# A seven-product FFN block whose two psum banks per unit become two tiles

## The chip, the cores and the metric

The kernel runs on one core of a Trainium2 chip. The metric is the device time of one execution, in microseconds (us). One profiled execution gives the trace; further runs are timed without it.

## What is computed

One backbone layer over 512 latent tokens and 256 context tokens, width 1024, with a feed-forward block (D_FF 2816) ahead of and behind a mixer of gated linear attention and differential attention. All weights are float32. The change lies in the first feed-forward block and in the adaLN modulation that is computed beside it:

```python
ml = jnp.split((jax.nn.silu(c) @ w_ada[i] + b_ada[i])[:, None, :], N_MOD, axis=-1)
mc = jnp.split((jax.nn.silu(c_ctx) @ w_ada[i] + b_ada[i])[None, None, :], N_MOD, axis=-1)

xl = xl + 0.5 * ml[2] * _swiglu(_modnorm(xl, ffn1_norm[i], ml[0], ml[1]), ffn1_w1[i], ffn1_w3[i], ffn1_w2[i])
xc = xc + 0.5 * mc[2] * _swiglu(_modnorm(xc, ffn1_norm[i], mc[0], mc[1]), ffn1_w1[i], ffn1_w3[i], ffn1_w2[i])

def _swiglu(h, w1, w3, w2):
    return (jax.nn.silu(h @ w1) * (h @ w3)) @ w2
```

## The kernel before, in words

A float32 number is split into a high part (rounded, by a copy on ScalarE) and the rest (by a subtraction on VectorE); a product of two split matrices is three matmuls: low by high, high by low, high by high. So each weight tile passes `split_w`: `whi<-raw` on ScalarE, then `wlo<-raw,whi` on VectorE.

**Units.** The 22 tiles of the inner dimension of the first feed-forward block are taken in pairs. The first pair is computed in a plain loop over k (`psum2`, `act_pair`). Each of the ten other pairs gives two units of class `Unit`: `i` = 0 for w1, `i` = 1 for w3, so units 0 to 19, in this order. A unit forms the four outputs of a 2 by 2 block product (two tiles by two token halves of TH = 384) from seven products instead of eight. A product (`prod`) is 12 matmuls of 128x384 into one psum bank. Three banks are in use: `pa` and `pf`, the first 384 columns of bank 0 and of bank 1 of one tile `st` of two banks, and `pe`, a tile of its own. `pa` accumulates and is copied by ScalarE at three points: p1 into `pa`, copy c1; p6 into `pa`, copy c2; p7 into `pa`, copy c3; p4 into `pa`. p5 and p3 go into `pf`, p2 into `pe`. The outputs are out(3) = c3 + `pf` (before p3), out(0) = c1 + `pe`, out(2) from `pa` after p4, and out(1) = c2 + `pf` after p3. For `i` = 0 VectorE adds and ScalarE applies Silu to give `s` (for out(2) ScalarE alone, `s<-st`); for `i` = 1 VectorE adds (`c<-c,st`), multiplies into `s` (`s<-st,s` for out(2)), ScalarE copies `gh<-s` and VectorE forms `gl`, the split gated result.

**What runs beside it.** Units 2, 3, 4, 5, 8, 9, 12, 13, 16 and 17 carry Down work (`Down`, products `dn` of the second weight with finished gated results, four output tiles each): ScalarE scales each result into a tile `yd`, and a DMA on GpSimd's queue adds it to `xs` in DRAM. `ada_dot` (line 129) gives the modulation: a 512 KB row block `adaw` is loaded by SP's queue and VectorE multiplies and sums it, in one or two products of 128x1024; 56 loads, 80 products, some in each Down unit.

**Order.** In a unit without Down work p4, out(2), p3 and out(1) are left to the next unit: p1, p5, then the earlier unit's p4, out(2), p3, out(1), then p6, p2, p7. In a unit with Down work all seven run: p1, p5 (the earlier unit's p4 and p3, if left), p6, Down, p7, Down, p2, p4, p3. Unit matmuls, copies, splits and outputs are kept in program order (`Kept`, the trace shows them all at line 496); the ada products and the loads are placed among them by the scheduler. An engine executes its instructions in order. Dependences are followed tile by tile: an instruction that writes a tile waits for what still reads it, whichever columns or banks the two touch.

The loop over units is at lines 659 to 732; `psum` (541) makes the tile, `out` (585) and `copy` read it, `Down.add` (650) makes `yd`.

Of the kernel before, what the change touches and what calls it, by code (L numbers as in the profile page):

```python
# [10 lines left out]
F32 = mybir.dt.float32  # L11
# [3 lines left out]
AF = mybir.ActivationFunctionType  # L15
ALU = mybir.AluOpType
AX = mybir.AxisListType
PSUM = bass.MemoryType.PSUM
DRAM = bass.MemoryType.DRAM

P = 128
D = 1024
# [3 lines left out]
T = TL + TC  # L26
# [4 lines left out]
TH, LH, CH = T // 2, TL // 2, TC // 2  # L31
# [27 lines left out]
def layer(tc, a, out, dump=None, stop=None):  # L59
    nc = tc.nc  # L60
    V, S, G, PE, SY = nc.vector, nc.scalar, nc.gpsimd, nc.tensor, nc.sync
    es = ExitStack()

    def pool(name, bufs=1, **kw):
        return es.enter_context(tc.tile_pool(name=name, bufs=bufs, **kw))
# [1 line left out]
    cst = pool("cst")  # L67
    wp = pool("wp")
    hp = pool("hp")
    ps = pool("ps", space=PSUM)  # L70
    dr = pool("dr", space=DRAM)

    def big(nm):
        return ps.tile([P, 1024], F32, tag="big", name=nm, bufs=2)

    def sm(nm):
        return ps.tile([P, 512], F32, tag="sm", name=nm, bufs=2)

    def gm(nm):
        return ps.tile([P, 512], F32, tag="gm", name=nm, bufs=2)  # L80

    uid = [0]

    def u(s):
        uid[0] += 1
        return f"{s}{uid[0]}"
# [35 lines left out]


    def ada_dot(pool_, junk, sc, j, which):
        w = pool_.tile([P, D], F32, tag="adaw", name=u("adaw"), bufs=3)
        SY.dma_start(w, a["ada"][j - 16])
        for i in which:
            jk = junk()
            V.scalar_tensor_tensor(jk, w, 1.0, sc[:, i, :], op0=ALU.mult, op1=ALU.mult,  # L129
                                   accum_out=mods[:, j, i:i + 1])  # L130
# [208 lines left out]
    h1 = Parts(B)  # L339
    h1.at = lambda i, k, o0, n: B[k // 4 * 2 + o0 // TH][i][:, k % 4, :]  # L340

    def psum2():
        t = [big(u("h13")) for _ in range(2)]
        return t, [(lambda o0, n, q=q: q[:, o0 // TH * 512:o0 // TH * 512 + TH]) for q in t]

    with tc.tile_pool(name="st", bufs=1) as sp_:
        scT = sp_.tile([P, KT, 32], F32, name="scT")
# [9 lines left out]
        pts, ds = psum2()  # L357
# [64 lines left out]
    def act_pair(f, pts):  # L422

        gh, gl = ring[f]
        s, p1, p3 = sums()[:, :T].rearrange("p (t n) -> p t n", t=2), *[q.rearrange("p (t n) -> p t n", t=2)[:, :, :TH] for q in pts]
        S.activation(s, p1, AF.Silu)
        V.tensor_tensor(s, s, p3, op=ALU.mult)
        S.activation(gh, s, AF.Copy)
        V.tensor_tensor(gl, s, gh.bitcast(F32), op=ALU.subtract)

    def sums():
        return sf.tile([P, D], F32, tag="Y", name=u("Y"), bufs=1)
# [11 lines left out]
    pts, ds = psum2()  # L444
# [64 lines left out]
    class Unit:  # L509
# [29 lines left out]
            self.S4 = split_w(self.a, spare[0][:, :512], spare[0][:, 512:])  # L539

        def psum(self):
            t = big(u("st"))
            self.pa, self.pf, self.pe = t[:, :TH], t[:, 512:512 + TH], sm(u("pe"))[:, :TH]
            if self.i == 0:
                ss[self.p] = sp0.tile([P, 4, TH], F32, tag="s", name=u("s"), bufs=1)
            self.s = ss[self.p]
# [82 lines left out]
    class Down:  # L629
# [20 lines left out]
        def add(self, j):  # L650
            m = self.m0 + j
            w = self.w[m - m % self.mw]
            y = sr.tile([P, 2, TH], F32, tag="yd", name=u("yd"), bufs=2)
            for i, seg in enumerate((LAT, CTX)):
                o_ = down(*CHUNKS1[self.c], w, m % self.mw * self.nf * P, seg, kPE)
                kS.activation(y[:, :, seg[0]], o_, AF.Copy, scale=gate[:, i, m:m + 1])
            G.dma_start(xs[:, m], y, accum_op=ALU.add)
# [77 lines left out]
    ada_bias(5, 9, (0,))  # L735
    ada_es.close()
    sf_es.close()
    V.tensor_scalar(gate[:, 2, :], mods[:, 40:48, 0], 0.5, None, op0=ALU.mult)
    V.tensor_scalar(gate[:, 3, :], mods[:, 64:72, 0], 0.5, None, op0=ALU.mult)
    mod_scale(2, V_MIX, 4, 0)  # L740
# [122 lines left out]
    with tc.tile_pool(name="dqp", bufs=1) as dq:  # L863
# [130 lines left out]
        st = {}  # L994
# [598 lines left out]
```

## Time and profile before

| what | value |
|---|---|
| median of 3 runs | 1896.28 us (1895.37 to 1898.03) |
| profiled execution | 1893.73 us |
| its span | 1891.9 us |
| mean granted TensorE clock | 0.969 |
| TensorE busy | 1738.4 us (92%) |
| VectorE busy | 1106.1 us (58%) |
| ScalarE busy | 750.9 us (40%) |

The units run from 86 to 663 us of the span. A wait is read as the idle time in front of an instruction and what ended it. The granted clock is the share of full speed that the throttle gave TensorE: 1.00 is 2.4 GHz, 0.50 is 1.2 GHz. Of a group of matmuls in a timeline row, "x12" counts those that follow each other without a stop.

### The profile page before, as it was taken

The numbers are of one execution on the slowest core, as the hardware profiler recorded it, in microseconds if no ns is written. First come the engines' busy times: TensorE is split into PE (matmuls) and PEld (weight loads), VectorE is DVE, ScalarE is ACT, GpSimd is POOL, SyncE is SP. The second block draws the span as 40 slices with busy tenths as digits, with TensorE's granted clock in tenths as the row PEclk, the third lists the DMA queues.
The fourth block names the chain that finished last, engine by engine and source line by source line (L and its number), as shares of the span: only waits on it lengthen the run. The fifth ranks groups of instructions, "written<-read, shape, count | busy, mean of one in ns | idle before, by whom it ended". The sixth has DMA issues, their size and how long they took to land.

```text
span 1891.9 us, 25078 instructions
## 1 busy us (share of the span) xinstructions
PE 1738.4 (92%) x9944; PEld 1552.4 (82%) x9944; DVE 1106.1 (58%) x1836; ACT 750.9 (40%) x1172; POOL 154.5 (8%) x244
## 2 busy tenths in 40 slices
PE   6787988878789879999999979999999999999997
PEld 4776877878778768989988879999888988888887
DVE  4775655565454566677765577668656743333335
ACT  4533333333233333455556463434333432222233
POOL 3022000100001021000000022112100200000000
PEclk9899999989899899999999999999999999999999
DMA  9347644636455055433432211211355322333231
GB/s 357 106 146 146 155 116 122 156 113 174 122 162 109 23 186 162 112 90 93 108 101 84 78 34 57 67 57 34 112 172 173 100 80 81 108 85 107 87 113 66
DMA packets 76486, 215.46 MB, mean 114 GB/s; under 512 B 9880, under 2 KB 14232, under 8 KB 75040
## 3 DMA queue, kind: packets, MB, share of 16 engines
q1 hardware_dynamic: 70608, 198.12, 33.3%
q0 software_dynamic: 5760, 15.73, 5.8%
q8 instruction: 78, 1.28, 0.3%
q14 instruction: 40, 0.33, 0.1%
HBM read 175.02 MB, written 27.26 MB: 107 GB/s over the span
## 4 chain that ended last, share of the span: by engine, by line
PE 67%; issue 17%; DVE 6%; DMA 4%; ACT 4%; POOL 2%; SPq 0%; DVEq 0%; ACTq 0%; POOLq 0%
PE h L248 8%; PE pl L248 8%; PE st L496 5%; PE h L245 4%; PE pl L245 4%; PE pb L248 3%; PE ptm L837 3%; PE ptm L836 3%; PE ptm L838 3%; PE S L945 2%; PE dn L496 2%; PE dn L119 2%; PE dn L121 2%; PE dn L120 2%; PE po L248 2%
## 5 line engine op out<-in xcount | busy, mean ns | idle before, releaser
L113 ACT ACTIVATE whi<-raw 128x1024 fp32r<-128x1024 f32 (+3 forms) x182 | 178.3, 983 | 264.5 <-PE dn L121 68.0
L114 DVE TENSOR_TENSOR wlo<-raw,whi 128x1024 fp32r<-128x1024 f32 (+3 forms) x169 | 191.2, 1135 | 151.0 <-ACT whi L113 149.6
L248 PE MATMUL h<-hH,whi 128*128 128x512 f32 (+2 forms) x384 | 145.3, 378 | 0.0
L248 PE MATMUL h<-hL,whi 128*128 128x512 f32 (+2 forms) x384 | 145.0, 378 | 0.0
L245 PE MATMUL h<-hH,wlo 128*128 128x512 f32 (+2 forms) x368 | 139.9, 381 | 1.9 <-ACT hH L401 0.9
L245 PE MATMUL pl<-hH,wlo 128*128 128x512 f32 x328 | 132.0, 402 | 10.0 <-DVE sg L1170 5.5
L248 PE MATMUL pl<-hL,whi 128*128 128x512 f32 x328 | 130.8, 399 | 0.0
L248 PE MATMUL pl<-hH,whi 128*128 128x512 f32 x328 | 130.5, 398 | 0.0
L496 PE MATMUL st<-T,whi 128*128 128x384 f32 x480 | 128.1, 349 | 0.0
L837 PE MATMUL ptm<-wlo,hH 128*128 128x256 f32 x384 | 109.7, 286 | 5.3 <-DVE wlo L114 5.3
L836 PE MATMUL ptm<-whi,hL 128*128 128x256 f32 x384 | 111.0, 290 | 0.0
L496 PE MATMUL st<-T,wlo 128*128 128x384 f32 x240 | 85.9, 358 | 27.3 <-ACT c L496 27.3
L838 PE MATMUL ptm<-whi,hH 128*128 128x256 f32 x384 | 109.4, 285 | 0.0
L496 PE MATMUL dn<-gh,wlo 128*128 128x512 f32 (+1 forms) x288 | 98.7, 343 | 10.0 <-ACT yd L496 10.0
L496 PE MATMUL st<-hC,hH 128*128 128x384 f32 x240 | 57.3, 397 | 50.2 <-DVE s L496 41.1
L129 DVE SCALAR_TENSOR_TENSOR Y<-adaw,sc 128x1024 f32<-128x1024 f32 x80 | 97.8, 1223 | 9.0 <-DMA adaw<-ada 8.1
L496 PE MATMUL dn<-gl,whi 128*128 128x512 f32 (+1 forms) x288 | 98.6, 342 | 1.0 <-DVE gl L496 1.0
L496 PE MATMUL dn<-gh,whi 128*128 128x512 f32 (+1 forms) x288 | 98.2, 341 | 0.0
L496 PEld LDWEIGHTS st<-hC,hH 128*128 128x128 f32 x240 | 49.8, 225 | 56.6 <-DVE s L496 44.3
L496 PEld LDWEIGHTS st<-T,whi 128*128 128x128 f32 x480 | 92.0, 199 | 0.0
L947 ACT ACTIVATE e<-S,st 128x768 f32<-128x768 f32 x64 | 57.6, 901 | 67.9 <-DVE st L946 67.8
L496 ACT ACTIVATE yd<-dn,gate 128x512 f32<-128x512 f32 x80 | 45.5, 580 | 98.1 <-PE dn L496 73.3
(351 smaller groups left out, 4592.2 us busy)
## 6 DMA issues: line engine op xcount, KB each, us to landing
raw<-win SPq DMA_DIRECT2D x65, 512.0 KB, 3.6
adaw<-ada SPq DMA_DIRECT2D x56, 512.0 KB, 4.3
raw<-f2w SPq DMA_DIRECT2D x44, 512.0 KB, 3.5
xs<-yd POOLq DMA_DIRECT2D x40, 384.0 KB, 5.1
raw<-f1w SPq DMA_DIRECT2D x22, 512.0 KB, 4.1
L<-f1w SPq DMA_DIRECT2D x40, 256.0 KB, 3.3
aw<-ada SPq DMA_DIRECT2D x8, 1024.0 KB, 14.5
raw<-wbr SPq DMA_DIRECT2D x16, 512.0 KB, 3.6
```

The lines of the kernel that those rows point to most:

```text
L113: S.activation(hi[:, :w], raw[:, :w], AF.Copy)
L114: ld = (eng or V).tensor_tensor(lo[:, :w], raw[:, :w], hi[:, :w].bitcast(F32), op=ALU.subtract)
L119: PE.matmul(out_, wl, xh, start=first, stop=False)
L120: PE.matmul(out_, wh, xlo, start=False, stop=False)
L129: V.scalar_tensor_tensor(jk, w, 1.0, sc[:, i, :], op0=ALU.mult, op1=ALU.mult, accum_out=mods[:, j, i:i + 1])
L245: PE.matmul(dst(o0, n), wl[:, ks], h.at(0, k, o0, n), start=(k == 0), stop=False)
L248: mm = PE.matmul(dst(o0, n), wh[:, ks], h.at(i, k, o0, n), start=False, stop=(k == KT - 1 and i == 0))
L496: return lambda *x, **y: tc.keep_in_program_order(f(*x, **y))
L836: PE.matmul(o_, tl, wh[:, cs], start=f, stop=False)
L837: PE.matmul(o_, th, wl[:, cs], start=False, stop=False)
L838: PE.matmul(o_, th, wh[:, cs], start=False, stop=l)
L947: S.activation(e[:, c, :], sp[:, :T], AF.Exp, bias=st4[:, c:c + 1], accum_out=st4[:, 2 + c:3 + c])
```

## The change

`bank(tag)` makes tiles of one bank, "ba" and "bf", two buffers each; `psum` of a unit takes `pa` and `pf` from them, and `psum2` of the first pair likewise. The four tags of psum live in a pool `ps1` that is closed behind the units; a new pool `ps` serves the rest of the kernel. `act_pair` works on each token half by itself, since its two banks are no longer one tile. `adaw` has two buffers instead of three, `yd` three instead of two. Names of lines move by four or five (L496 becomes L501, L129 becomes L130).

```diff
--- before.py
+++ after.py
@@ -67,17 +67,18 @@
     cst = pool("cst")
     wp = pool("wp")
     hp = pool("hp")
-    ps = pool("ps", space=PSUM)
+    ps_es = ExitStack()
+    psb = [ps_es.enter_context(tc.tile_pool(name="ps1", bufs=1, space=PSUM))]
     dr = pool("dr", space=DRAM)
 
     def big(nm):
-        return ps.tile([P, 1024], F32, tag="big", name=nm, bufs=2)
+        return psb[0].tile([P, 1024], F32, tag="big", name=nm, bufs=2)
 
     def sm(nm):
-        return ps.tile([P, 512], F32, tag="sm", name=nm, bufs=2)
+        return psb[0].tile([P, 512], F32, tag="sm", name=nm, bufs=2)
 
     def gm(nm):
-        return ps.tile([P, 512], F32, tag="gm", name=nm, bufs=2)
+        return psb[0].tile([P, 512], F32, tag="gm", name=nm, bufs=2)
 
     uid = [0]
 
@@ -122,7 +123,7 @@
 
 
     def ada_dot(pool_, junk, sc, j, which):
-        w = pool_.tile([P, D], F32, tag="adaw", name=u("adaw"), bufs=3)
+        w = pool_.tile([P, D], F32, tag="adaw", name=u("adaw"), bufs=2)
         SY.dma_start(w, a["ada"][j - 16])
         for i in which:
             jk = junk()
@@ -339,9 +340,12 @@
     h1 = Parts(B)
     h1.at = lambda i, k, o0, n: B[k // 4 * 2 + o0 // TH][i][:, k % 4, :]
 
+    def bank(tag):
+        return psb[0].tile([P, 512], F32, tag=tag, name=u(tag), bufs=2)[:, :TH]
+
     def psum2():
-        t = [big(u("h13")) for _ in range(2)]
-        return t, [(lambda o0, n, q=q: q[:, o0 // TH * 512:o0 // TH * 512 + TH]) for q in t]
+        t = [[bank(tag) for tag in ("ba", "bf")] for _ in range(2)]
+        return t, [(lambda o0, n, q=q: q[o0 // TH]) for q in t]
 
     with tc.tile_pool(name="st", bufs=1) as sp_:
         scT = sp_.tile([P, KT, 32], F32, name="scT")
@@ -422,9 +426,10 @@
     def act_pair(f, pts):
 
         gh, gl = ring[f]
-        s, p1, p3 = sums()[:, :T].rearrange("p (t n) -> p t n", t=2), *[q.rearrange("p (t n) -> p t n", t=2)[:, :, :TH] for q in pts]
-        S.activation(s, p1, AF.Silu)
-        V.tensor_tensor(s, s, p3, op=ALU.mult)
+        s = sums()[:, :T].rearrange("p (t n) -> p t n", t=2)
+        for t in range(2):
+            S.activation(s[:, t], pts[0][t], AF.Silu)
+            V.tensor_tensor(s[:, t], s[:, t], pts[1][t], op=ALU.mult)
         S.activation(gh, s, AF.Copy)
         V.tensor_tensor(gl, s, gh.bitcast(F32), op=ALU.subtract)
 
@@ -539,8 +544,7 @@
             self.S4 = split_w(self.a, spare[0][:, :512], spare[0][:, 512:])
 
         def psum(self):
-            t = big(u("st"))
-            self.pa, self.pf, self.pe = t[:, :TH], t[:, 512:512 + TH], sm(u("pe"))[:, :TH]
+            self.pa, self.pf, self.pe = bank("ba"), bank("bf"), sm(u("pe"))[:, :TH]
             if self.i == 0:
                 ss[self.p] = sp0.tile([P, 4, TH], F32, tag="s", name=u("s"), bufs=1)
             self.s = ss[self.p]
@@ -650,7 +654,7 @@
         def add(self, j):
             m = self.m0 + j
             w = self.w[m - m % self.mw]
-            y = sr.tile([P, 2, TH], F32, tag="yd", name=u("yd"), bufs=2)
+            y = sr.tile([P, 2, TH], F32, tag="yd", name=u("yd"), bufs=3)
             for i, seg in enumerate((LAT, CTX)):
                 o_ = down(*CHUNKS1[self.c], w, m % self.mw * self.nf * P, seg, kPE)
                 kS.activation(y[:, :, seg[0]], o_, AF.Copy, scale=gate[:, i, m:m + 1])
@@ -735,6 +739,8 @@
     ada_bias(5, 9, (0,))
     ada_es.close()
     sf_es.close()
+    ps_es.close()
+    psb[0] = pool("ps", space=PSUM)
     V.tensor_scalar(gate[:, 2, :], mods[:, 40:48, 0], 0.5, None, op0=ALU.mult)
     V.tensor_scalar(gate[:, 3, :], mods[:, 64:72, 0], 0.5, None, op0=ALU.mult)
     mod_scale(2, V_MIX, 4, 0)
```

The matmuls of the units stand in the same order as before. What moves is what they wait for, and where the ada products stand on VectorE. In the rows below numbers tell one buffer of a name from another.

TensorE at the end of unit 13 (Down, `i` = 1): p3 of unit 13 into the second bank, then p1 of unit 14. Before:

```order
L496 MATMUL st_3420<-hC_93,hH_91 128x384 [waits DVE_49]
L496 MATMUL st_3420<-hC_93,hH_91 128x384 x11
L496 MATMUL st_3719<-hH_91,wlo_3658 128x384
L496 MATMUL st_3719<-hH_91,whi_3657 128x384 [waits Activation_49]
L496 MATMUL st_3719<-hH_91,whi_3657 128x384
L496 MATMUL st_3719<-hH_91,wlo_3658 128x384
```

and of the changed kernel:

```order
L501 MATMUL bf_3442<-hC_93,hH_91 128x384 [waits DVE_49]
L501 MATMUL bf_3442<-hC_93,hH_91 128x384 x11
L501 MATMUL ba_3741<-hH_91,wlo_3680 128x384 [waits DVE_49]
L501 MATMUL ba_3741<-hH_91,whi_3679 128x384 [waits Activation_49]
L501 MATMUL ba_3741<-hH_91,whi_3679 128x384
L501 MATMUL ba_3741<-hH_91,wlo_3680 128x384
```

p3's wait on VectorE is before for the `s` that out(2) forms from the first bank; now it is for `c` of out(3), the last reader of the second bank, and p1 has got a wait of its own for the weights' `wlo`.

TensorE from the last matmuls of unit 14's p1 into its p5. Before:

```order
L496 MATMUL st_3719<-hH_91,wlo_3658 128x384
L496 MATMUL st_3719<-hH_91,whi_3657 128x384 x2
L496 MATMUL st_3719<-T_564,wlo_3658 128x384 [waits Activation_49]
L496 MATMUL st_3719<-T_565,whi_3657 128x384
L496 MATMUL st_3719<-T_564,whi_3657 128x384
L496 MATMUL st_3719<-T_564,wlo_3658 128x384
L496 MATMUL st_3719<-T_565,whi_3657 128x384
```

and of the changed kernel:

```order
L501 MATMUL ba_3741<-hH_91,wlo_3680 128x384
L501 MATMUL ba_3741<-hH_91,whi_3679 128x384 x2
L501 MATMUL bf_3742<-T_570,wlo_3680 128x384
L501 MATMUL bf_3742<-T_571,whi_3679 128x384
L501 MATMUL bf_3742<-T_570,whi_3679 128x384
L501 MATMUL bf_3742<-T_570,wlo_3680 128x384
L501 MATMUL bf_3742<-T_571,whi_3679 128x384
```

p5 (`T,wlo` and on) waited for ScalarE's copy c1 of the first bank and now waits for nothing; p6, which follows p5 here and writes the first bank, waited for nothing and now waits for c1 and for its weights.

VectorE at the end of unit 11 (left over into unit 12, which has Down work): out(2) into `s`, out(1) into `c` and `s`, the splits `hC`, `hH` of the unit's weights, with the ada products `Y<-adaw` between. Before:

```order
L129 SCALAR_TENSOR_TENSOR Y_3327,mods<-adaw_3325,sc 128x1024 [waits DMAHW0_49,DVE_49]
L496 TENSOR_TENSOR wlo_3130<-raw_3104,whi_3129 128x1024 [waits DMAHW2_49,PE_49,Activation_49]
L129 SCALAR_TENSOR_TENSOR Y_3331,mods<-adaw_3329,sc 128x1024 [waits DMAHW1_49,DVE_49]
L129 SCALAR_TENSOR_TENSOR Y_3365,mods<-adaw_3363,sc 128x1024 [waits DMAHW2_49,DVE_49]
L129 SCALAR_TENSOR_TENSOR Y_3369,mods<-adaw_3367,sc 128x1024 [waits DMAHW3_49,DVE_49]
L496 SCALAR_TENSOR_TENSOR s_2875<-st_2970,s_2875 128x384 [waits PE_49]
L496 TENSOR_TENSOR hC_93<-L_2973,hL_92 128x1024 [waits Activation_49]
L496 TENSOR_TENSOR gl_3098<-s_2875,gh_3097 128x384 [waits DVE_49]
L496 TENSOR_TENSOR c_3053<-c_3053,st_2970 128x384 [waits PE_49]
L496 TENSOR_TENSOR s_2875<-s_2875,c_3053 128x384 [waits DVE_49]
L496 TENSOR_TENSOR hH_91<-A_2974,hH_91 128x512 [waits Activation_49]
L496 TENSOR_TENSOR gl_3078<-s_2875,gh_3077 128x384 [waits DVE_49]
```

and of the changed kernel:

```order
L130 SCALAR_TENSOR_TENSOR Y_3293,mods<-adaw_3291,sc 128x1024 [waits DMAHW7_49,DVE_49]
L501 TENSOR_TENSOR wlo_3151<-raw_3125,whi_3150 128x1024 [waits DMAHW1_49,PE_49,Activation_49]
L501 SCALAR_TENSOR_TENSOR s_2894<-ba_2989,s_2894 128x384 [waits PE_49]
L130 SCALAR_TENSOR_TENSOR Y_3348,mods<-adaw_3346,sc 128x1024 [waits DMAHW0_49,DVE_49]
L501 TENSOR_TENSOR hC_93<-L_2993,hL_92 128x1024 [waits Activation_49]
L501 TENSOR_TENSOR gl_3118<-s_2894,gh_3117 128x384 [waits DVE_49]
L501 TENSOR_TENSOR c_3073<-c_3073,bf_2990 128x384 [waits PE_49]
L130 SCALAR_TENSOR_TENSOR Y_3352,mods<-adaw_3350,sc 128x1024 [waits DMAHW1_49,DVE_49]
L501 TENSOR_TENSOR s_2894<-s_2894,c_3073 128x384 [waits DVE_49]
L130 SCALAR_TENSOR_TENSOR Y_3386,mods<-adaw_3384,sc 128x1024 [waits DMAHW3_49,DVE_49]
L501 TENSOR_TENSOR hH_91<-A_2994,hH_91 128x512 [waits Activation_49]
L501 TENSOR_TENSOR gl_3098<-s_2894,gh_3097 128x384 [waits DVE_49]
```

Ada products that stood ahead of out(2)'s `s` now stand behind it, between out(2) and the `gl` of out(1); there are three between them where there were none.

## Rows read from the trace of the kernel before

**Rows 1.** The page's head: span and number of instructions.
```profile
span 1891.9 us, 25078 instructions
```

**Rows 2.** Unit stage: length, busy time (instructions) by engine, granted clock, DMA share, GB/s.
```profile
86.00:663.00 577.00, 485.74 (x2558) 450.86 (x2559) 324.66 (x489) 203.61 (x322) 48.50 (x56) 0.93 0.50 127
```

**Rows 3.** Waits in 86 to 663 us: engine, awaited; us in all, times, longest.
```profile
PE st L496 <- DVE s L496: 41.1, 10, 6.6
...
PE st L496 <- ACT c L496: 27.3, 20, 4.4
...
ACT yd L496 <- DMA xs<-yd: 18.8, 5, 5.6
...
PE dn L496 <- ACT yd L496: 10.0, 7, 3.2
PE st L496 <- ACT s L496: 9.1, 10, 1.2
...
DVE Y L129 <- DMA adaw<-ada: 8.1, 11, 1.4
...
PE st L496 <- DVE c L496: 1.2, 1, 1.2
```

**Rows 4.** Half-clock windows, TensorE: length, busy (instructions), granted clock, DMA share; their sum.
```profile
486.42:489.83 3.41, 3.41 (x9) 0.50 0.76 107
504.28:510.31 6.03, 6.03 (x19) 0.50 0.00 0
...
sum 56.76, PE 56.75; mean PE 4.37
```

**Rows 5.** Timeline, TensorE: start, us, operation, count, idle before and its end.
```profile
552.03 2.37 PE L496 MATMUL st<-hC,hH 128*128 128x384 f32 x12 [2.14 <-DVE s L496]
```

**Rows 6.** Timeline behind unit 13, the same columns.
```profile
503.67 0.55 DVE L496 SCALAR_TENSOR_TENSOR s<-st,s 128x384 f32<-128x384 f32 x1
504.25 0.52 ACT L496 ACTIVATE gh<-s 128x384 fp32r<-128x384 f32 x1 [2.23 <-DVE s L496]
...
504.28 4.21 PE L496 MATMUL st<-hC,hH 128*128 128x384 f32 x12 [6.56 <-DVE s L496]
...
511.50 0.49 ACT L496 ACTIVATE c<-st 128x384 f32<-128x384 f32 x1 [1.27 <-PE st L496]
...
512.05 0.44 PE L496 MATMUL st<-T,wlo 128*128 128x384 f32 x1 [0.58 <-ACT c L496]
```

**Rows 7.** Timeline in unit 4: the first Down weights' low part, the first Down product.
```profile
200.16 1.22 DVE L496 TENSOR_TENSOR wlo<-raw,whi 128x1024 fp32r<-128x1024 f32 x1
...
202.75 0.39 PE L496 MATMUL dn<-gh,wlo 128*128 128x512 f32 x1
```

**Rows 8.** Timeline in unit 12: p5, the last ada product, out(1)'s `gl`, a Down product.
```profile
420.78 0.44 PE L496 MATMUL st<-T,wlo 128*128 128x384 f32 x1 [4.39 <-ACT c L496]
...
428.78 1.23 DVE L129 SCALAR_TENSOR_TENSOR Y<-adaw,sc 128x1024 f32<-128x1024 f32 x1 [1.41 <-DMA adaw<-ada]
...
436.60 0.55 DVE L496 TENSOR_TENSOR gl<-s,gh 128x384 fp32r<-128x384 f32 x1
...
437.76 0.39 PE L496 MATMUL dn<-gh,wlo 128*128 128x512 f32 x1
```

**Rows 9.** The page's groups and DMA issues: the ada products, the loads of `adaw`.
```profile
L129 DVE SCALAR_TENSOR_TENSOR Y<-adaw,sc 128x1024 f32<-128x1024 f32 x80 | 97.8, 1223 | 9.0 <-DMA adaw<-ada 8.1
...
adaw<-ada SPq DMA_DIRECT2D x56, 512.0 KB, 4.3
```

**Rows 10.** Timeline at the stage's end: out(1) of unit 19.
```profile
659.83 0.56 DVE L496 TENSOR_TENSOR c<-c,st 128x384 f32<-128x384 f32 x1 [0.56 <-PE st L496]
```

## The prediction

> **What bounds the kernel now.** I read the page's head first, then busy time by stage, then the waits of the stage that the change touches, then the windows of half clock, then the timeline around the longest waits. The profiled execution spans 1891.9 us [rows 1] and took 1893.73 us, 1.83 us around the span; it lies 2.55 us under the median of the runs, 1896.28 us. The sum is made on the profiled execution and then moved by these 2.55 us.
>
> The change works almost wholly in the unit stage, 86 to 663 us. There TensorE is busy 485.74 of 577 us, VectorE 324.66 and ScalarE 203.61, and the granted clock is 0.93 [rows 2]: no engine is full, so TensorE waits for results, some 91 us in all. The waits say for what [rows 3]: 41.1 us for VectorE's `s` (10 times) and 9.1 us for ScalarE's `s` (10 times), both in front of p3; 27.3 us for ScalarE's copy `c` (20 times), in front of p5; 10.0 us for `yd`, of which ScalarE itself waited 18.8 us for the DMA out of `yd`. The waits of p3 and p5 are waits on the other half of the same tile: p3 writes `pf` in bank 1 while out(2) reads `pa` in bank 0, and p5 writes `pf` while c1 is read from `pa`.
>
> Behind long waits the clock falls. The windows that follow waits of 2.66 us and more stand at a granted clock of 0.50, the lower of the two levels, 1.2 GHz; 13 of them hold 56.76 us of matmuls [rows 4], which at 2.4 GHz would take half, so they cost 28.4 us. The wait of 2.14 us had none behind it: the p3 there took 2.37 us for its twelve matmuls [rows 5], the one at 504.28 took 4.21 [rows 6]. The Trainium skill (TensorE: Matmul & The Clock Gate, "Terms") puts the penalty at throttled time times the share of pulses withheld; with the stage's mean clock of 0.93 [rows 2] that would be some 40 us, an estimate, and the first rival below would end 12 us lower. Against it: in its throttled time lie the waits themselves, in which no matmul is slowed. I stay with the 28.4 us of the busy rows.
>
> **The change part by part, its places in the order of the sum.**
>
> *p5, eleven places.* Twenty p5 waited 27.3 us; four took 4.4 us (17.6 us, one is in [rows 8]), so sixteen share 9.7 us, 0.6 each. Five of these stand behind a Down unit and are counted there. In the changed program c1's copy is needed at p6, a product later, and nothing else of p5's stands behind it. Twelve matmuls at full clock take some 2.1 us, and the copy 0.49 us [rows 6], so p5 hides it. Eleven times 0.6: **6.7 us**.
>
> *p3 of the i = 0 units.* Ten waits on ScalarE's Silu, 9.1 us [rows 3]. Now p3 waits for out(3)'s read of the second bank, which lies before p4. What is late next is p6, a product behind p3: it follows c1, and c1 stood ahead of the Silu. **9.1 us**.
>
> *From a Down unit with i = 1 to the next unit (five places).* Take 497.7 us: p4 has ended, p3 waits 6.56 us for `s`, starts at 504.28, and runs at half clock with the next p1; p5 then waits 0.58 us and starts at 512.05 [rows 6]; p6 could follow 2.1 us later, at 514.1. Why is `s` late? Not for p4: out(2)'s `s` stands on VectorE behind c3, out(3), the split of the next weights, out(0) and the split of Y. That order stays. So after the change TensorE runs p3, p1 and p5 from 497.7 to 504.0 and then stops at p6. p6 writes `pa` over c1's source, and c1 stands on ScalarE behind the `gh` of out(2) and of out(1). The chain from the row at 503.67: `s` to 504.22, `gl` behind `gh` to 505.4, `c` to 506.0 and `s` to 506.5 (p3 is long done), `gh` 0.52 to 507.0, c1 to 507.4. A gap of 3.4 us, and by the 2.66 us above half clock behind it: 3.4 to 6.0 us of matmuls in such windows [rows 4], so 1.7 to 3.0 us; I take 2.0. p6's work is then 514.1 − 507.4 − 2.0 = 4.7 us earlier. I take this for four places. At the fifth Down work follows: its first product needs `wlo`, begun at 200.16, and started at 202.75 [rows 7]; one ada product fewer lies ahead of `wlo` now, so it comes a little over 1 us earlier, to 200.3; less half of a short clock window I take 1.8. Together 4 × 4.7 + 1.8 = **20.6 us** of the 50 us (6.6 + 0.6 + 2.8 of clock, five times) that these places lose now. Bounds: 10 us where a clock window of 6 us stands behind each and c1 is later by 1 us, 35 us where the clock stays.
>
> *From a plain i = 1 unit to a Down unit (four places).* Here three ada products stand ahead of `s`, the last after 1.41 us for its load, and the Down product for the third f tile starts at 437.76, one microsecond after `gl` of out(1) [rows 8]. The waits at p5 (4.4) and at p3 go. But TensorE then arrives at the third tile about 9 us early, at 428.5, and must have that `gl`. On VectorE one to four ada products move from ahead of `s` to behind it, with three still between `s` and `gl`; from the durations (1.31 us each, `hC` 1.2, `hH` 0.7, three of 0.6) `gl` comes to 431 to 434. The gap there is 3 to 5 us, with a clock window behind it of 2 us. Per place 437.8 − 434 − 2.0 = 1.8 at the late end, 4.8 at the early one, and nothing where loads hold the products up. I take 0.5 each, near the bad end for the loads' sake (next part): **2 us**, between −6 and 18.
>
> *adaw with two buffers, yd with three.* A buffer of `adaw` is loaded in 4.3 us and read in 1.22 us [rows 9], 1.31 with the read of the accumulator: three buffers give a load every 1.9 us, two every 2.8. VectorE waited 8.1 us for such loads [rows 3]. Most of what is added meets an idle VectorE (252 us in the stage) and costs nothing; some 3 us of it stand in the chains above, which is why I took their bad end. Behind a waiting product are queued `s`, `gl` and the splits, and TensorE's Down work and next unit wait for these. Loads of `raw`, `L` and `A` stand earlier on SP's queue than before, a gain if anything. With three `yd`, ScalarE no longer waits for the DMA of two tiles ago: of the 10.0 us three waits, 6.6 us (3.2 the longest), go, and two clock windows of 3.4 us behind them (one is 486.42 [rows 4]) give 3.4: **10 us**, between 5 and 12.
>
> *Ends and the small parts.* At the end p4 no longer waits 1.2 us for `c` [rows 3] but 0.6 for the copy, and p3's 0.65 goes. In return the first Down product of the new pool waits until out(1) has read its bank, 659.83 + 0.56 [rows 10], 0.8 us later than it started. **0.5 us** gained. act_pair in halves adds two ScalarE and two VectorE instructions of about half a microsecond each, as the copies and products of one half are [rows 6]: at worst 2.1 us, at best a gain since the second half overlaps the first. I take **−0.3**. The banks as tiles cost no instruction; the matmuls' order in the units is the same.
>
> Sum: 6.7 + 9.1 + 20.6 + 2 + 10 + 0.5 − 0.3 = 48.6 us. 1893.73 − 48.6 = 1845.1 for the profiled execution, plus 2.55: **1847.7 us**.
>
> **Rivals.**
> 1. *Nothing new is late.* If the chain on VectorE is hurried by the earlier products, all of 41.1 + 9.1 + 27.3 + 6.6 us and the clock of twelve windows (26.9) go: 111 us, 1785 us. Against it: `s` is late by its own chain, not by p3, as the rows at 503.67 show. Half of it, 80 us, is 1816. The waits of the unit stage would then show almost none over 2 us.
> 2. *The chain takes nearly all back.* p6 and the Down products wait as long as p3 and p5 did, with half clock behind them; what stays are the short waits, 6.7 + 9.1, and half of `yd`, 5: 21 us, 1875. For it: the VectorE order in a unit is the same in both programs. The Trainium skill (same page, "A second HAM failure mode: psum-queue depth-cycling") warns that short stops between groups of matmuls keep throwing the clock down; by it the forecast's own short gaps would cost clock too, and this rival would be the likelier. The trace speaks against it: behind the stop of 2.14 us the clock stayed up [rows 5].
> 3. *Slower: two `adaw` buffers.* If each of the 56 loads stands in the chain, it costs 0.93 us each, 52 us, against 48.6 gained; with a landing of 5.1 us (the two buffers then give one every 3.2 us, three every 2.1) it is 60 us, 1908 us. It decides from 3.9 us of landing on with all loads exposed, or from 9.1 us with half of them. Against it: VectorE stands still for 252 us of the stage, and only 11 of 80 products waited at all [rows 3].
> 4. *The tiles change no wait*, since the reader is the later one anyway: then only `yd` gives, 10 us, 1886. Against it: the order of instructions shows p5 with no wait and p3 with another one.
>
> **How the numbers follow.** My forecast 70%, the first rival 10%, the second 13%, the third 4%, the fourth 3%. The range reaches up to the second rival's inner half (1872) and down to the first rival's (1818); by the bounds of the terms alone, 20 us off the five places and 16 off the four, it would be about as wide. What a measurement of this kernel can tell from no change is about 0.2%, 3.8 us. Faster by more: all but the third rival and a rest where the second goes further, 0.93; same 0.03; slower 0.04.
>
> **What would show it.** Right: in the profile after, no wait of p3 and none of p5; p6 (`T,wlo` into the first bank) waits for ScalarE's `c` about 3 us at five places; Down products wait for `gl` or `gh` at four places; waits for `yd` on DMA nearly gone; busy TensorE time in the unit stage lower by 10 to 18 us through the clock. Wrong: p3 still waits for `s`; VectorE's waits for `adaw` above 30 us; p6's waits above 6 us, which would mean that c1 hangs on more than the two `gh`; or unit waits so short that the clock stays up.

## The result and the profile after

The changed kernel took 1838.22 us (median of 4 runs, 1835.12 to 1842.8) beside 1896.2 us for the kernel before (4 runs): a ratio of 0.9695, 95% interval 0.9672 to 0.9717, 58 us less. I had forecast 1847.7 us, 48.6 us less, with a range of 1818 to 1872. The profiled execution took 1835.12 us.

The page's head and the line of the engines, for [rows 1]; then, of the view by stretch, the unit stage, which now ends at 607.6 us ([rows 2]: length, busy time of PE, PEld, DVE, ACT and POOL with instructions, granted clock, DMA share, GB/s):

```profile
span 1833.3 us, 25087 instructions
...
PE 1719.7 (94%) x9944; PEld 1541.1 (84%) x9944; DVE 1104.5 (60%) x1838; ACT 750.0 (41%) x1174; POOL 157.4 (9%) x244
```

```profile
86.00:607.60 521.60, 470.89 (x2558) 442.77 (x2559) 323.65 (x489) 201.95 (x321) 50.97 (x56) 0.94 0.56 142
```

The same 2558 matmuls take 521.6 us instead of 577: 14.9 us less busy time, which is clock and the starts behind stops, and some 40 us less idle time. The waits of the stage, for [rows 3] (engine, awaited; us in all, times, longest):

```profile
DVE Y L130 <- DMA adaw<-ada: 28.2, 15, 4.2
...
PE ba L501 <- ACT c L501: 20.4, 6, 5.9
...
PE dn L501 <- ACT gh L501: 14.7, 3, 5.3
...
PE dn L501 <- ACT yd L501: 8.0, 5, 6.1
PE ba L501 <- DVE wlo L501: 7.8, 1, 7.8
...
PE dn L501 <- DVE gl L501: 2.8, 3, 1.0
PE pe L501 <- DVE hC L501: 1.4, 3, 0.5
```

No wait of p3 and none of p5 is left: `bf` is in no row. What is late now are p6 (`ba` for `c`), the Down products for `gh`, `gl` and `yd`, and, on VectorE, the ada products for their loads. (The one wait of 7.8 us for `wlo` stands in front of the first unit, where it was 5.9 us before.) Two of the new stops in TensorE's timeline, behind unit 13 for [rows 6] and in unit 12 for [rows 8] (start, us, operation, count, idle before and what ended it):

```profile
403.63 0.79 PE L501 MATMUL dn<-gh,wlo 128*128 128x512 f32 x1 [4.69 <-ACT gh L501]
405.35 0.80 PE L501 MATMUL dn<-gl,whi 128*128 128x512 f32 x1 [0.92 <-DVE gl L501]
...
469.40 0.44 PE L501 MATMUL ba<-T,wlo 128*128 128x384 f32 x1 [3.47 <-ACT c L501]
...
473.70 0.44 PE L501 MATMUL pe<-hL,hC 128*128 128x384 f32 x1 [0.46 <-DVE hC L501]
```

p6 stops for 3.47 to 3.48 us behind four of the Down units, where I had worked out 3.4, and for 5.9 us behind the fifth, unit 3. The Down product of the third f tile stops for 4.69 us, where I had 3 to 5, and 0.92 us more for `gl`. The small stop of 0.46 us in front of p2, for `hC`, turned out to be the more telling row.

### The profile page after: what moved, and what is told of

The parts are those of the page before. It is cut to its first block, busy times and chain, and to the rows that moved or that the text cites. A ratio compares the mean times of both kernels' runs of the same rounds, so it can differ in the third digit from the quotient of the medians.

```text
span 1833.3 us, 25087 instructions
## 1 busy us (share of the span) xinstructions
PE 1719.7 (94%) x9944; PEld 1541.1 (84%) x9944; DVE 1104.5 (60%) x1838; ACT 750.0 (41%) x1174; POOL 157.4 (9%) x244
## 4 chain that ended last, share of the span: by engine, by line
PE 76%; DVE 11%; ACT 5%; issue 4%; DMA 3%; POOL 1%; DVEq 0%; SPq 0%; ACTq 0%; POOLq 0%
PE h L249 8%; PE pl L249 8%; PE dn L501 7%; PE ba L501 5%; PE h L246 4%; PE pl L246 4%; PE pb L249 3%; PE ptm L843 3%; PE ptm L842 3%; PE ptm L844 3%; PE S L951 3%; PE dn L120 2%; PE dn L122 2%; PE dn L121 2%; PE bf L501 2%
## 5 line engine op out<-in xcount | busy, mean ns | idle before, releaser
L246 PE MATMUL h<-hH,wlo 128*128 128x512 f32 (+1 forms) x352 | 133.6, 380 | 0.0
L249 PE MATMUL h<-hL,whi 128*128 128x512 f32 (+1 forms) x352 | 133.5, 379 | 0.0
L249 PE MATMUL h<-hH,whi 128*128 128x512 f32 (+1 forms) x352 | 133.5, 379 | 0.0
L501 PE MATMUL dn<-gh,wlo 128*128 128x512 f32 (+1 forms) x288 | 101.5, 353 | 23.8 <-ACT gh L501 14.7
L130 DVE SCALAR_TENSOR_TENSOR Y<-adaw,sc 128x1024 f32<-128x1024 f32 x80 | 97.7, 1221 | 29.0 <-DMA adaw<-ada 28.2
L501 PE MATMUL dn<-gl,whi 128*128 128x512 f32 (+1 forms) x288 | 101.0, 351 | 2.8 <-DVE gl L501 2.8
L501 PE MATMUL dn<-gh,whi 128*128 128x512 f32 (+1 forms) x288 | 100.2, 348 | 0.0
L501 PE MATMUL ba<-T,whi 128*128 128x384 f32 x320 | 87.8, 357 | 0.0
L501 ACT ACTIVATE yd<-dn,gate 128x512 f32<-128x512 f32 x80 | 45.8, 582 | 98.7 <-PE dn L501 94.4
L501 PEld LDWEIGHTS dn<-gh,wlo 128*128 128x128 f32 x288 | 57.2, 199 | 33.1 <-ACT gh L501 15.9
L246 PEld LDWEIGHTS pl<-hH,wlo 128*128 128x128 f32 x328 | 62.0, 189 | 23.2 <-issue 5.4
L843 PEld LDWEIGHTS ptm<-wlo,hH 128*128 128x128 f32 x384 | 75.3, 196 | 6.3 <-DVE wlo L115 5.9
L246 PEld LDWEIGHTS h<-hH,wlo 128*128 128x128 f32 x352 | 66.2, 188 | 12.5
```

Source lines behind the costliest of these rows:

```text
L246: PE.matmul(dst(o0, n), wl[:, ks], h.at(0, k, o0, n), start=(k == 0), stop=False)
L249: mm = PE.matmul(dst(o0, n), wh[:, ks], h.at(i, k, o0, n), start=False, stop=(k == KT - 1 and i == 0))
L501: return lambda *x, **y: tc.keep_in_program_order(f(*x, **y))
L843: PE.matmul(o_, th, wl[:, cs], start=False, stop=False)
```

## The experiments

All are set against runs of the kernel before on the same chip, and told as ratios, since that kernel's median differed between chips (1891.5 to 1896.2 us). Of the longer edits the main lines are shown, and `...` marks what is left out. A place's gain is read in the traces by the start of the same matmul in both.

### The three parts apart

**split_only**: one-bank tiles alone, buffers as before.

```diff
-        w = pool_.tile([P, D], F32, tag="adaw", name=u("adaw"), bufs=2)
+        w = pool_.tile([P, D], F32, tag="adaw", name=u("adaw"), bufs=3)
...
-            y = sr.tile([P, 2, TH], F32, tag="yd", name=u("yd"), bufs=3)
+            y = sr.tile([P, 2, TH], F32, tag="yd", name=u("yd"), bufs=2)
```

> The changed kernel with the buffers of before: one-bank tiles, adaw three buffers, yd two. My theory: the waits of p5 and p3 go by the tiles alone, and the third yd gives about 10 us, so this run stands some 10 us above the changed kernel (1838.2 us), less what a third adaw buffer spares, 0 to 5 us: 1843 to 1850 us, and waits of Down products for yd are back, about 7 to 10 us with half clock behind the longest. Rival: the third yd carries much more of the gain: 1860 us or above. Rival: two adaw buffers cost the changed kernel much: below 1838 us.

**split_2_2**: one-bank tiles, two buffers for both (of the diff above only the second pair of lines).

> The changed kernel with yd back to two buffers, adaw two. Against the changed kernel it gives the price of yd alone: my theory 10 us, so 1846 to 1850 us. Against the run with three adaw buffers it gives the price of the third adaw buffer: my theory 0 to 5 us; the rival in which adaw loads decide says over 10 us.

**bufs_only**: the kernel before with `adaw` two and `yd` three.

> The kernel before with adaw two buffers and yd three, the two-bank tile kept. My theory: yd gives up to 10 us, two adaw buffers take some back since ada products stand ahead of out(2) in the chain that p3 waits for: 1886 to 1896 us, with p3's and p5's waits of 50 and 27 us still there or larger. Rival, two adaw buffers are dear: above 1900 us, VectorE's waits for adaw above 20 us. Rival, yd is worth more than its own waits: below 1886 us.

**before_adaw2**: the kernel before with `adaw` two and nothing else.

> The kernel before with two adaw buffers instead of three and nothing else. Against my prediction, two adaw buffers gained 7 us in the changed kernel (split_2_2 against split_only). Theory from those traces: fewer adaw loads in flight let the DMAs out of yd land sooner, so here the waits of Down products for yd of 0.7 and 2.7 us go and the 3.2 us in unit 2 stays, while VectorE's waits for adaw rise from 8 to 24 us without holding anything: 3 to 6 us below the kernel before, ratio 0.997 to 0.998. Rival, the loads in the chain cost time here, as I had predicted: equal or slower, ratio 1.000 to 1.003.

Measured:

| kernel | tile | adaw, yd | median us | ratio to before, 95% interval |
|---|---|---|---|---|
| before_adaw2 | two banks | 2, 2 | 1890.57 | 0.9985 (0.9967 to 1.0002) |
| bufs_only | two banks | 2, 3 | 1883.13 | 0.9953 (0.9939 to 0.9967) |
| split_only | one bank | 3, 2 | 1854.93 | 0.9812 (0.978 to 0.9845) |
| split_2_2 | one bank | 2, 2 | 1848.41 | 0.9776 (0.9754 to 0.9797) |
| changed kernel | one bank | 2, 3 | 1838.22 | 0.9695 (0.9672 to 0.9717) |
| changed kernel again (after_again) | one bank | 2, 3 | 1840.27 | 0.9723 (0.9695 to 0.975) |

The tiles alone (with `act_pair` in halves and the new pool, which come with them) give 1.9%, 36 us; I had expected at least 5 us more. With them, the step from three `adaw` buffers to two gave 6.5 us (1854.93 to 1848.41, same chip), where I had put a small cost and a rival. The intervals of these two ratios overlap a little, so the size is rough, and the traces below have to show the sign. The third `yd` gave 0.5 to 0.8%, 10 to 15 us, by the two measurements of the changed kernel. In the kernel before, the third `yd` gave some 6 us (the ratios 0.9985 and 0.9953), and for two `adaw` buffers alone no difference is shown: 3 us, with 1 inside the interval.

Why fewer `adaw` buffers gained can be read where the two traces still run side by side, in unit 9. The DMA issues of 341 to 343 us, first of split_only, then of split_2_2 (out<-in, queue, count, size, us from issue to landing):

```profile
adaw<-ada SPq DMA_DIRECT2D x2, 512.0 KB, 7.5
xs<-yd POOLq DMA_DIRECT2D x1, 384.0 KB, 9.8
```

```profile
adaw<-ada SPq DMA_DIRECT2D x1, 512.0 KB, 5.4
xs<-yd POOLq DMA_DIRECT2D x1, 384.0 KB, 6.5
```

The same transfer out of `yd`, issued within 0.05 us of the same time, lands after 9.8 us beside two `adaw` loads issued there and after 6.5 us beside one. With two `yd` buffers the next scaling waits for that landing. The trace of split_only has forty such transfers, and by the loads' issues and landings in it the other transfers agree: the 25 with next to no load of `adaw` beside them land after 4.8 to 5.3 us, the twelve with the most beside them after 6.0 to 9.8. Over all forty the median is the same with two buffers (5.3 us, against 5.2); it is the longest that gets shorter, 8.2 us against 9.8. ScalarE's and TensorE's waits, of split_only:

```profile
ACT yd L501 <- DMA xs<-yd: 22.6, 4, 6.8
PE dn L501 <- ACT yd L501: 20.3, 8, 6.1
...
DVE Y L130 <- DMA adaw<-ada: 9.3, 6, 2.2
```

and of split_2_2:

```profile
DVE Y L130 <- DMA adaw<-ada: 26.4, 18, 3.4
ACT yd L501 <- DMA xs<-yd: 19.6, 5, 6.5
PE dn L501 <- ACT yd L501: 14.3, 6, 6.1
```

VectorE's waits for `adaw` rise by 17 us, and nearly all of that is hidden: the stop for `gh` in unit 8 grew from 5.29 to 5.69 us, and no other stop of TensorE grew by more. TensorE's waits for `yd` fall by 6: two stops, of 3.1 us in unit 9 and 2.7 in unit 13, are gone, and the way from p2 to p2 is 4.9 and 4.6 us shorter there.

These rows also show why the third `yd` is worth more behind the split than in the kernel before: TensorE now runs ahead into the transfers. Its stops for `yd` that stand behind a transfer had risen from 6.6 of the 10.0 us [rows 3] to 12.5 of the 20.3, and two `adaw` buffers bring them back to 6.5. In the changed kernel 8.0 us of waits for `yd` are left, none of them behind a transfer; most of that is one stop of 6.1 us in unit 2, where the scaling stands on ScalarE behind a late `gh`.

before_adaw2 bears this out in part only. Of the stops for `yd` of the kernel before, the one of 0.73 us is gone, the one of 2.66 is now 1.08, and the one of 3.2 stays (it stands in unit 3), much as expected; but one of 1.35 us in unit 2 has become 3.17, behind a transfer.

### What makes the stop behind a Down unit

**c1_first**: the next unit's p1 with its copy c1 is issued ahead of out(2) and out(1).

```diff
...
             un.p4()
-            un.out(2)()
-            un.p3()
+            if un.i and nx:
+                un.p3()
+                nx.psum()
+                nx.p1()
+                nx.early = True
+                un.out(2)()
+            else:
+                un.out(2)()
+                un.p3()
             un.out(1)()
```

> The changed kernel, but behind a Down unit with i = 1 the next unit's p1 and its copy c1 are issued ahead of out(2) and out(1), so that on ScalarE c1 stands ahead of both gh; TensorE's order is the same. My theory, that p6 stops because c1 is queued behind the two gh: p6's waits of 3.5 us at four places and 5.9 us at the fifth fall under 0.6 us and the half clock behind them goes, 20 to 24 us less: about 1816 us. Rival, the chain on VectorE is what is late and the stop only moves to p2 (for hC) or to the wlo of Y: 1830 us or above, with stops of 2 us or more there.

Measured: 1846.7 us, ratio 0.9761 (0.9742 to 0.978), slower than the changed kernel (0.9695 and 0.9723): the rival. The stop of p6 is gone, and this row stands in the waits instead, with the timeline behind unit 5 (at the fifth place, behind unit 3, the stop is now 5.0 us, at the first Down product, for `wlo`):

```profile
PE pe L501 <- DVE hC L501: 22.8, 4, 5.7
```

```profile
257.39 1.22 DVE L501 TENSOR_TENSOR hC<-L,hL 128x1024 fp32r<-128x1024 f32 x1
...
258.66 0.69 PE L501 MATMUL pe<-hL,hC 128*128 128x384 f32 x1 [5.70 <-DVE hC L501]
```

In the changed kernel p2 of the same unit starts at 258.71, and from the p2 before it takes 18.34 us in both, so the place has gained nothing: the limit is `hC` on VectorE, and c1 behind the `gh` was only the first thing in the way. The kernel even lost, and the clock shows why. Windows of TensorE in c1_first (length, busy with matmuls, granted clock, DMA share, GB/s):

```profile
258.66:261.50 2.84, 2.84 (x9) 0.50 0.68 190
261.50:264.50 3.00, 3.00 (x11) 0.50 0.83 256
264.50:267.50 3.00, 3.00 (x18) 1.00 0.02 7
```

and in the changed kernel:

```profile
254.41:256.50 2.09, 2.09 (x7) 0.60 0.00 0
256.50:258.71 2.21, 1.81 (x6) 0.61 0.00 0
258.71:261.50 2.79, 2.79 (x16) 1.00 0.65 199
```

There the stop comes one product earlier, the half clock falls on p6, which has time to spare before `hC`, and the full 2.4 GHz is back when p2 starts. In c1_first the half clock falls behind the limit, on p2 and p7, and from p2 to the next p2 costs 1.5 to 2.7 us at each of four places, against the profiled execution of 1835.12 us.

The changed kernel itself shows both cases. In the profiled execution of after_again p6 stops as long in the same unit, but runs at full clock, and p2 waits longer for `hC` (timeline, then windows of p6 and of p2's start):

```profile
254.55 0.44 PE L501 MATMUL ba<-T,wlo 128*128 128x384 f32 x1 [3.48 <-ACT c L501]
...
258.86 0.44 PE L501 MATMUL pe<-hL,hC 128*128 128x384 f32 x1 [1.95 <-DVE hC L501]
```

```profile
254.55:256.90 2.35, 2.35 (x12) 1.00 0.00 0
258.86:261.50 2.64, 2.64 (x10) 0.65 0.55 173
```

p2 comes no earlier for it: from the p2 before it takes 18.36 us, against 18.34 with p6 at half clock. The lower clock then falls behind p2, and the next p2 comes after 16.25 us, against 14.67. (So the clock did not fall at once behind every wait of 2.66 us and more, as I had read from [rows 4]: behind this one of 3.48 us a whole product ran at 2.4 GHz.)

**hc_first**: as c1_first, and the split of the next unit's L is issued ahead of out(2) too.

```diff
...
+                nx.split_l()
                 nx.early = True
                 un.out(2)()
...
```

> As c1_first, and the split of the next unit's L (hL on ScalarE, hC on VectorE) is issued ahead of out(2) too. The run c1_first showed the stop of p6 gone and one of 5.7 us at p2 for hC in its place. My theory now: what is late behind a Down unit is VectorE's queue, out(2), out(1), the split of the next X, hC, in this order; with hC ahead of them p2 is ready at 2 us after p6 begins and both stops go, only p1 of the unit after may wait up to 1 us for wlo: 18 to 24 us below the changed kernel on this chip. Rival, VectorE's queue as a whole is late there and TensorE runs into the next thing in it (wlo of the next X, in front of p1) with a stop of 3 us or more: under 8 us gained.

Measured: 1832.84 us, ratio 0.9686 (0.9657 to 0.9716), against 1840.27 us (0.9723) of the changed kernel beside it: 7 us, the rival's size. p2 starts 5.9 us earlier at each of four places, and 4.4 to 5.0 of it are given back by the next p2 (against after_again): p7 waits for c2, which stands behind both `gh`.

```profile
472.89 0.44 PE L501 MATMUL ba<-T,wlo 128*128 128x384 f32 x1 [3.26 <-ACT c L501]
```

**outs_last**: out(2) and out(1) behind the next unit's p6 as well, with a second buffer for c2.

```diff
...
         un.p6()
+        if un.late:
+            un.late.out(2)()
+            un.late.out(1)()
+            un.split_a()
+            un.take_s()
...
+                un.p3()
+                nx.psum()
+                nx.p1()
+                nx.split_l()
+                nx.late = un
...
```

> The changed kernel; behind a Down unit with i = 1, out(2) and out(1) are issued behind the next unit's p1, split of L, split of the following X and p6, with a second buffer for c2. So c1 and c2 stand ahead of both gh on ScalarE, and hC and wlo stand ahead of out(2) on VectorE. In hc_first the stop had moved on to p7 (3.3 us, for c2 behind the gh). My theory: the two queues hold some 17 us of work there, TensorE's eight products take 16.6 us, so nothing is late in itself and only the order makes the stops; now no stop of over 1 us is left between the Down unit and the second unit behind it, and the half clock there goes: 18 to 25 us below the changed kernel (0.969 to 0.972 of the kernel before), a ratio of 0.957 to 0.961. Rival, the two queues are late by their whole work and the stop comes back at the next thing (p1 or p3 of the unit after) with 3 us: no more than 8 us below.

Measured: 1830.65 us, ratio 0.9667 (0.9635 to 0.9698), by the ratios 0.3 to 0.6%, 5 to 11 us, under the changed kernel, where I had expected 18 to 25. The rival again: p2 is ahead by 5.9 us, and the stop comes back at the p4 that is left to the second unit.

```profile
449.78 0.55 DVE L501 TENSOR_TENSOR c<-c,bf 128x384 f32<-128x384 f32 x1 [1.60 <-ACT c L501]
...
471.54 0.55 DVE L501 TENSOR_TENSOR s<-c,pe 128x384 f32<-128x384 f32 x1
...
472.18 0.52 ACT L501 ACTIVATE s<-s 128x384 f32<-128x384 f32 x1 [1.81 <-DVE s L501]
472.61 0.47 ACT L501 ACTIVATE c<-ba 128x384 f32<-128x384 f32 x1
...
473.14 0.44 PE L501 MATMUL ba<-T,hC 128*128 128x384 f32 x1 [3.11 <-ACT c L501]
```

The rows are a chain. From out(3) at 449.78 to out(0) of the next unit at 471.54 VectorE goes through its whole queue; its only pauses are for ScalarE's half of a split or of a `gh` (0.4 to 1.1 us each). ScalarE's Silu waits for that `s`, c3 stands behind the Silu, and p4 waits for c3. So the chain of VectorE and ScalarE from out(3) on takes 23.4 us where TensorE needs 3.1 us less. Four orders, and the stop stood at p6 (3.47), p2 (5.70), p7 (3.26) and p4 (3.11): these orders moved it and shortened it little. That less work in the chain would take it away is what the rows suggest; no run tried it.

### What makes the stop in the Down product

**ada_behind**: in Down units with an earlier unit's outputs left over, ada products are issued behind the `gl` of out(1).

```diff
...
+            behind = low()
...
-                more_ada(ada.pop())
+                if behind is not None:
+                    with tc.issue_after(getattr(behind, "ins", behind)):
+                        more_ada(ada.pop())
+                else:
+                    more_ada(ada.pop())
```

> The changed kernel, with the ada products of a Down unit that has an earlier unit's outputs left over issued on VectorE behind the gl of out(1). My theory: the stops of 4.7 to 5.3 us in front of the third f tile (three places) and the 6.1 us for yd in unit 2 come from the three ada products between out(2) and that gl; they fall to 2 us or less and the half clock behind them goes: 12 to 20 us below the changed kernel. Rival, the gl is late by out(2) and the splits alone: stops stay above 3.5 us and less than 6 us is gained. Second rival, the products, each behind a load, now hold up wlo of the second Down weights or out(3): new stops there, nothing gained.

Measured: 1830.52 us, ratio 0.9672 (0.9647 to 0.9696), 9.8 us under the changed kernel on the same chip, less than the 12 to 20 expected. The stop at the third f tile fell as expected, the one in unit 2 only from 6.1 to 3.5 us, and a new one of 2.5 to 3.4 us came half a unit later at three places:

```profile
392.54 0.50 PE L501 MATMUL dn<-gl,whi 128*128 128x512 f32 x1 [1.22 <-DVE gl L501]
...
405.96 0.55 DVE L501 TENSOR_TENSOR s<-c,bf 128x384 f32<-128x384 f32 x1
406.54 0.53 ACT L501 ACTIVATE s<-s 128x384 f32<-128x384 f32 x1 [4.35 <-DVE s L501]
...
408.83 0.50 PE L501 MATMUL dn<-gh,wlo 128*128 128x512 f32 x1 [2.97 <-ACT yd L501]
```

out(3) of the unit, at 405.96, stands behind ada products that wait for loads; ScalarE waits 4.35 us for it, with the scaling into `yd` queued behind. The second rival held in part.

**both2**: hc_first and ada_behind together.

> The two changes of hc_first and ada_behind together. They work at different places, so the theory gives the sum of the two gains against the changed kernel, 30 to 44 us, some 1790 to 1805 us. If they share a cause (VectorE's queue as a whole), well under the sum.

Measured: 1826.3 us, ratio 0.9651 (0.9622 to 0.968): 14 us under the changed kernel. That is most of the sum of the two as measured (7.4 and 9.8), and far from the sum as expected.

**outs_last_ada**: outs_last and ada_behind together.

> outs_last and ada_behind together: the ada products behind the gl of out(1) in Down units that have an earlier unit's outputs left over. ada_behind alone took the stop at the third f tile from 4.7 to 1.2 us, 10 us in all, and brought a stop of 2.5 to 3.4 us for yd, since ScalarE's queue then waited for out(3) behind the ada products. Expected the sum of both: 28 to 35 us below the changed kernel, a ratio of 0.951 to 0.956. If the places are not independent, over 0.957.

Measured: 1821.82 us, ratio 0.962 (0.9587 to 0.9654). By the ratios 0.8 to 1.1%, 14 to 20 us, under the changed kernel; the fastest of all, but less than the 28 to 35 us expected. The stops of both parts that are left stand in its trace: 3.1 us at p4, 2.6 to 3.2 us for `yd`.

**outs_last_ada4**: outs_last, with all ada products of the Down units behind a plain unit, from unit 8 on, behind out(3).

> outs_last, and in the Down units behind a plain unit (from unit 8 on) all ada products are issued behind VectorE's part of out(3). My theory of the yd stop in ada_behind, that ScalarE waits in order for out(3)'s s, which stands behind the ada products: the 2.5 to 3.4 us for yd fall under 1 us and the stop at the third f tile stays at 1.2: 3 to 8 us below outs_last_ada. Rival: eight products in a row, each behind a load, hold up Y's split or out(0) of that unit: no gain over outs_last_ada, with new stops of p2 or p6 behind it.

Measured: 1840.8 us, ratio 0.9726 (0.9693 to 0.9758): the rival. The stop for `yd` is gone in these units, but the products in a row, most of them behind a load, hold up what the next unit needs; p6 of unit 13 then waits for c1, queued on ScalarE behind outputs that VectorE is late with (unit 17 has the same stop, of 9.7 us):

```profile
430.33 0.69 PE L501 MATMUL ba<-T,wlo 128*128 128x384 f32 x1 [9.34 <-ACT c L501]
```

## Why the prediction was right, and where it was not

By the start of the same matmul in both profiled executions the change gained 58.6 us. By place, taken from p2 to p2:

| place | forecast | measured |
|---|---|---|
| Down unit, i = 1, to the next unit (5) | 20.6 | 20.1 |
| plain unit to Down unit (4) | 2 | 3.7 |
| p5 and p3 elsewhere, yd, act_pair | 6.7 + 9.1 + 10 − 0.3 = 25.5 | 31.0 |
| end of the units | 0.5 | 0.6 |
| behind the units | 0 | 3.2 |

Against the profiled execution of after_again, the same kernel, the first three rows are 19.2, 3.2 and 28.6 and the last two together −0.2 instead of 3.9. So the first two rows are good to about 1 us, the others to 2 to 4.

**The five places behind Down units** came out near the forecast: 4.1 to 4.6 us at four (4.7 forecast) and 2.4 at the fifth (1.8). The chain `s`, `gl`, `c`, `s`, `gh`, c1 from [rows 6] gave the stop to 0.1 us. The step "c1 stands behind the two `gh`" was true and yet not what bounds the place, as c1_first showed: `hC` let p2 start up to 0.5 us after the end of a p6 that ran at about half clock, and 1.95 us after the end of one that ran at full clock (after_again). So the 2.0 us that I took off for half clock stood for a wait for `hC`, and that the two agree to some tenths is luck; with the clock up in p6, as in my bound of 35 us, p2 came no earlier. At the fifth place I had the Down product's wait for `wlo` as the limit, and what stopped was p6, for 5.9 us: ada products stood between the outputs that c1 waits behind.

**The plain units ahead of Down units**: at three of the four places stops of 4.67 to 5.3 us where I had 3 to 5, and 0.9 us behind them for `gl`, with ada products in the chain as ada_behind confirmed; at the fourth the 6.1 us in unit 2. The places gained 2.6, 1.9, 0.6 and −1.4 us where I took 0.5 each. That their sum is near is no more than the middle of a wide spread.

**p5, p3 and the third yd** were under-sized by 5.5 us. A stop costs more than its idle time. From p2 of unit 18 to p2 of unit 19 before, with the two stops between:

```profile
632.50 0.33 PE L496 MATMUL pe<-hL,hC 128*128 128x384 f32 x1
...
639.54 0.44 PE L496 MATMUL st<-T,wlo 128*128 128x384 f32 x1 [0.64 <-ACT c L496]
...
644.56 2.35 PE L496 MATMUL st<-hC,hH 128*128 128x384 f32 x12 [0.58 <-ACT s L496]
...
648.83 0.34 PE L496 MATMUL pe<-hL,hC 128*128 128x384 f32 x1
```

and after, without them:

```profile
579.42 0.44 PE L501 MATMUL pe<-hL,hC 128*128 128x384 f32 x1 [0.53 <-DVE hC L501]
...
594.10 0.33 PE L501 MATMUL pe<-hL,hC 128*128 128x384 f32 x1
```

16.33 us became 14.68: 1.65 us for 1.22 us of idle time, 0.2 us more for each stop. At the eight distances that had short stops alone the gain is 4.0 us more than the idle time, between −0.1 and 0.9 us each: most of the 5.5. The others were not shown one by one, and 2.4 of the 5.5 are gone in after_again.

**The step that failed is adaw.** I had two buffers as a cost in the chain, and as the rival on the slower side. In the split kernel the sign is the other one, some 6.5 us gained; the loads in flight cost more by what they do to the transfers out of `yd` than by VectorE's waits for them. These waits rose as I had thought (8.1 to 28.2 us) and were mostly hidden. The 10 us for `yd` held only because two things that I had not seen met: the split made TensorE's waits behind transfers twice as long (6.6 to 12.5 us), and two `adaw` buffers took that back (6.5) before the third `yd` took the rest.

**The rivals.** Nothing came near the first; the second, that the chain takes nearly all back, is largely true of the further orders tried here (hc_first and outs_last gave 5 to 11 us of 18 to 25), and not of the change: behind four of the Down units stops of 7.1 us in all became 3.5 to 4.0, and the half clock behind them fell where `hC` hid it. The clock term was about right: TensorE's busy time in the stage fell by 14.9 us, within the 10 to 18 forecast, part of it the starts behind stops.

Three figures of the working are loose without moving the forecast. Halfway between the forecast and the first rival is 80 us; half of that rival would be 56. By its own figures the bound "where the clock stays" is 6.7 us a place, 33.5 and not 35. And the two bounds lie 11 and 14 us from the term of the five places, where the range speaks of 20.

The 3.2 us behind the units were not forecast: 1.5 us in the stop and the clock at the stage's end, 1.7 us in stretches that the change does not touch but for the new pool. The latter are no gain of the change as far as can be told: the two executions of the changed kernel differ by 3.7 us in the same stretches, as the last section shows for one of them.

## What to carry to other kernels

A wait on a tile of several banks is a wait on all that reads any of them; make a tile of each bank that has its own readers, and write down what each write will then wait for, since it is the next thing in an in-order queue that sets the gain. Work out that next thing through the queues of all engines, not only the one that is named: here VectorE's `hC`, needed one product later, set the pace and not the copy that the trace named, and four orders mainly moved the stop. And count loads in flight as a cost to other transfers: one buffer fewer for an early load gained some 6.5 us in the split kernel, and in the kernel before nothing that could be told.

## What the runs showed of the hardware

Where a stop falls matters as much as its length: half clock behind a stop that lay ahead of another late input cost nothing here, and behind the last late input 1.5 to 2.7 us a place (c1_first, and after_again against the first profiled execution of the changed kernel, windows above). And the granted clock differs between executions of one kernel in a stretch with the same instructions. The view by stretch of the changed kernel's two profiled executions, from a later stage that no part of the change touches, first the one of 1835.12 us, then, of after_again, the one of 1843.0 us:

```profile
946.00:1118.00 172.00, 162.62 (x1004) 143.97 (x1004) 109.76 (x208) 90.30 (x138) 18.33 (x45) 0.95 0.21 68
```

```profile
950.00:1126.00 176.00, 167.16 (x1007) 147.62 (x1006) 110.22 (x209) 90.31 (x138) 18.38 (x45) 0.93 0.21 66
```

4.5 us more busy time for nearly the same matmuls (4.2 for the same 1003), at a clock of 0.93 instead of 0.95, while VectorE's and ScalarE's busy time agree to 0.5 us. This stretch makes up 3.6 of the 7.9 us between these two executions, and a difference of 3 us between two single executions is not to be explained.
